# Stick-breaking attention on one NeuronCore: the carries of both heads in the two halves of one tile, and the work of a unit in one row

## The chip, the cores and the metric

The kernel runs on one NeuronCore of a Trainium2 chip. The time is the device time of one execution in microseconds (us); where several executions were timed, their median is given. The profile is of one further execution, and its span runs from that execution's first instruction to its last.

The engines are named as in the profile: PE multiplies matrices (PEld is the loading of its stationary operand), DVE is the vector engine, ACT the scalar engine, POOL the general engine, and SP issues most of the transfers.

## The reference, cut to what matters

The kernel computes one decoder block on 1024 rows of width 1024: a state-space branch and an attention branch, joined by gates, and a feed-forward part. The change lies in the attention of 8 heads with 64 dimensions each, of which this is the core:

```python
z = jnp.einsum('bhqd,bhkd->bhqk', qb, kh) * scale
mask = key_pos < q_pos
log_not = jnp.where(mask, jax.nn.log_sigmoid(-z), 0.0)
suffix = lax.cumsum(log_not, axis=3, reverse=True) - log_not
weights = jnp.where(mask, jnp.exp(jax.nn.log_sigmoid(z) + suffix), 0.0)
return jnp.einsum('bhqk,bhkd->bhqd', weights, vh)
```

So a weight needs the sum of `log_not` over all keys that lie behind it. The kernel goes through the keys from the last to the first and hands the sum so far from one block of 128 keys to the next. That handed-on sum is what the code keeps in the tiles `row0` and `row1`; it is called the carry here.

## The kernel before, in words

Before the attention come the projections and the state-space branch (to about 345 us of the span), after it the output projection of the branch and the gates (`branch_b`, from about 642 us), the output matrix, and the feed-forward part. The program is built by a framework that orders the instructions of DVE, ACT, POOL and SP by its own estimate of times. The matrix products of the attention are kept in the order in which the code writes them: all of them go through `pinned` (line 838), so in the profile the line of every one of them is L838, and they are told apart by the names of their tiles.

The attention goes through four pairs of heads. Of each pair, the 64 dimensions of one head lie in rows 0 to 63 of the operands `q` and `k`, those of the other in rows 64 to 127. Of each pair there are two groups of 512 queries (Q = 0 and 1), and each group goes through its blocks of keys from the last to the first, three units in the first group and seven in the second: 40 units in all. The first unit of a group holds the two last blocks, with 128 and 256 queries behind the mask; the second has 384 queries, all others 512.

A unit passes through three functions, at different times:

- `scores`: products of `k` and `q` into the PSUM tile `z`, one per head (64 rows each). Then a copy on ACT (L920), or on DVE with the mask added (L918) for the three blocks on the diagonal, and on ACT and DVE the steps to `ws`, which DVE splits into a high part `wh` (L925) and a rest `wl` (L926), in fp32r, the rounded float format in which one pass of PE suffices.
- `sums`: for each head two products of `upto`, a triangle of ones, with `wh` and `wl` into the PSUM tile `acc`, and, from a group's second unit on, one product of `ones` with the carry. The carry tile holds 128 rows and both heads beside each other, [128, 2, 512]. Only two of its rows are not zero: row 0 (high part) and row 32 (rest), so that one product with all 128 rows of ones adds both. Then the new carry is taken from row 0 of `acc`: ACT writes its high part for both heads in one instruction (L947), DVE subtracts `acc` from the scores of each head (L949, twice) and writes the rest of the carry for both heads (L951). The tile `acc` is there once, so the next unit's sums wait for L951. ACT then takes the exponential (L952), which gives the weights `wa`.
- `values`: products of the weights and `V` into a PSUM tile named `mm`, one per head, 64 columns of the array each.

PE doesn't run these alone. Between them stand products of other projections (the next heads' `q` and `k`, the gates), called fillers, by counts in `FILL`. In the loop of `attention`, step i writes: the sums of unit i, 8 fillers, the values of unit i-1, the scores of unit i+3, 8 fillers. In the last three steps there are no scores any more, and 8 and 6 fillers. For the fillers, POOL splits weights into high parts and rests (L458, L459).

Of the kernel before, what the change touches and what calls it, by code (L numbers as in the profile page):

```python
# [9 lines left out]
F32 = mybir.dt.float32  # L10
F32R = mybir.dt.float32r
I32 = mybir.dt.int32
AF = mybir.ActivationFunctionType
ALU = mybir.AluOpType
# [350 lines left out]
P = 128  # L365
# [12 lines left out]
LOOK = 3  # L378
FILL = (8, 8, 12, 6)
# [50 lines left out]
class Block:  # L430
# [497 lines left out]
    def sums(self, u, work):  # L928


        nc, g, a, f = self.nc, u.group, u.a, u.f
        kb, fs, c = u.segs[-1]
        past = g.row
        r = self.accp.tile([P, 2, 512], F32, name="acc")
        for x in range(2):
            for n in range(2):
                self.pinned(r[:, x, 0:f], lhsT=self.upto, rhs=u.parts[n][:, x, 0:f], start=n == 0, stop=False)
            if past is None:
                for n in range(2):
                    self.pinned(r[:, x, f - P:f], lhsT=self.ones_r, rhs=u.parts[n][:, x, 0:P], start=False, stop=n == 1)  # L940
        if past is not None:
            old = slice(c.start + P if kb >= 4 * u.Q else 0, 512)
            for x in range(2):
                self.pinned(r[:, x, old.start - c.start:f], lhsT=self.ones_r, rhs=past[:, x, old], start=False, stop=True)
        if kb:
            g.row = self.rows.tile()
            nc.scalar.copy(g.row[0:1, :, c], r[0:1, :, fs])  # L947
        for x in range(2):
            nc.vector.tensor_tensor(a[:, x, 0:f], a[:, x, 0:f], r[:, x, 0:f], ALU.subtract)  # L949
        if kb:  # L950
            nc.vector.tensor_tensor(g.row[32:33, :, c], r[0:1, :, fs], g.row[0:1, :, c].bitcast(F32), ALU.subtract)  # L951
        self.last_exp = nc.scalar.activation(a[:, :, 0:f], a[:, :, 0:f], AF.Exp)  # L952

    def values(self, u, out):
# [9 lines left out]
    def attention(self, qk, qp, kp, vp, op, gp, rowp, part, work, cp):  # L964


        nc = self.nc
        units, ops = [], []
        carries = []
        for n in range(RWB):  # L970
            t = rowp.tile([P, 2, 512], F32R, name=f"row{n}")
            carries.append(t)
        self.rows = Again(carries)
        for hp in range(4):
# [6 lines left out]
        def some(n):  # L981
            for _ in range(n):
                next(fill, None)

        V = None
        for i in range(-LOOK, len(units) + 1):
            if 0 <= i < len(units):
                self.sums(units[i], work)
                some(FILL[0])
            if i > 0:  # L990
                u = units[i - 1]
                if u.group.av is None:
                    if u.Q == 0:
                        V = vp.tile([P, KT, P], F32, name="V")
                        nc.sync.dma_start(out=V, in_=self.vD.rearrange("(t p) d -> p t d", p=P)[:, :, P * u.hp:P * u.hp + P])
                        ops.append(op.tile([P, 1024], F32, name="o"))
                    u.group.V = V
                    u.group.av = self.avp.tile([P, 512], F32, name="mm")
                self.values(u, ops[u.hp])
            if i + LOOK < len(units):  # L1000
                self.scores(units[i + LOOK], qk, part, work)
                if i == -LOOK:
                    for t in carries:
                        self.after(nc.vector.tensor_scalar(t.rearrange("p a (b c) -> p (a b) c", c=P), self.ident.unsqueeze(1).broadcast_to([P, 8, P]), 0.0, None, ALU.mult), self.masked)
                some(FILL[1] if i >= 0 else FILL[2])
            elif i < len(units):
                some(FILL[3])
        some(10000)
        return ops

# [607 lines left out]
```

## Time and profile before

| | |
|---|---|
| median of three runs | 1433.7 us (1431.09 to 1435.74) |
| profiled execution, its own time | 1436.13 us |
| its span | 1434.4 us |
| PE busy | 1408.1 us, 98% of the span |
| DVE busy | 1078.4 us, 75% |
| ACT busy | 639.9 us, 45% |
| POOL busy | 514.5 us, 36% |
| granted clock of PE | 0.996 |

The view of stretches gives the busy time of each engine between two times; the timeline gives instructions in order, those of a kind that follow each other merged with their number (x2); the view of groups gives for each form its count, its busy time and the mean duration of one, and behind the bar the idle time just before them. A product of two f32 operands shows as two instructions, one of two fp32r operands as one. On PE the durations of neighbours overlap, so a product's price is read from one start to the next, not from its duration.

### The profile page before, as it was taken

Reading aid. Unit: us, or ns where it says so; the run is one execution under the profiler, and the core shown is the slowest. Engines: PE = TensorE matmul, PEld = TensorE weight load, DVE = VectorE, ACT = ScalarE, POOL = GpSimd, SP = SyncE. Lnnn points to the kernel's source line nnn. Section 1 sums busy time; section 2 is a strip of 40 time slices with the busy share of each in tenths; the row PEclk is TensorE's granted clock in tenths of the full one; section 3 lists DMA queues with packets and bytes.
Section 4 is the critical chain, followed back from the end, with each engine's and each line's share of the span. In section 5 each row is a group of like instructions: output and inputs, shape, how many; then the busy total and the mean of one; then the engine's idle time right before and its main releaser. Section 6 shows DMA issues by size and latency. Waiting matters only on the chain.

```text
span 1434.4 us, 18472 instructions
## 1 busy us (share of the span) xinstructions
PE 1408.1 (98%) x6821; PEld 1121.3 (78%) x6821; DVE 1078.4 (75%) x1388; ACT 639.9 (45%) x852; POOL 514.5 (36%) x288
## 2 busy tenths in 40 slices
PE   8899999998999999999999999999999999999997
PEld 6689888887666666668888888888888888788886
DVE  5679985656897989877824697877667667799896
ACT  4433324423777776774328442332323233433335
POOL 1020000102101111104400017776767666699394
PEclk9999999999999999999999999999999999999999
DMA  9656667299011112217533234444444359899722
GB/s 338 170 136 178 161 161 213 69 334 310 16 52 52 44 30 81 66 38 240 190 121 118 68 91 152 167 139 162 140 162 138 117 198 386 287 370 364 253 81 117
DMA packets 193274, 233.41 MB, mean 163 GB/s; under 512 B 29468, under 2 KB 128864, under 8 KB 193184
## 3 DMA queue, kind: packets, MB, share of 16 engines
q1 hardware_dynamic: 184048, 224.70, 47.8%
q10 hardware_dynamic: 8912, 7.48, 1.9%
q8 instruction: 54, 0.88, 0.3%
q14 instruction: 36, 0.29, 0.1%
q0 software_dynamic: 224, 0.05, 0.0%
HBM read 162.85 MB, written 68.16 MB: 161 GB/s over the span
## 4 chain that ended last, share of the span: by engine, by line
PE 80%; DVE 9%; DMA 5%; ACT 3%; issue 2%; POOL 1%; SPq 0%; ACTq 0%; POOLq 0%; DVEq 0%
PE tq L1308 12%; PE wo L1308 6%; PE tq L1429 6%; PE mm L1308 6%; PE mx L838 5%; PE mm L838 5%; PE mm L767 4%; PE mm L1429 3%; PE mx L767 3%; PE wo L1429 3%; PE acc L838 2%; PE wo L1145 2%; PE mm L1145 2%; PE mm L664 2%; PE z L838 2%
## 5 line engine op out<-in xcount | busy, mean ns | idle before, releaser
L475 POOL TENSOR_TENSOR ws<-wb 128x1024 f32<-128x1024 f32 x24 | 60.6, 2526 | 171.4 <-DVE wl L478 142.7
L459 POOL TENSOR_TENSOR wl<-ws,wh 128x1024 fp32r<-128x1024 f32 x12 | 31.4, 2616 | 151.4 <-ACT wh L456 150.9
L949 DVE TENSOR_TENSOR wa<-wa,acc 128x512 f32<-128x512 f32 (+1 forms) x80 | 47.0, 628 | 31.0 <-ACT row L947 28.8
L1355 POOL TENSOR_TENSOR pa<-pa 128x512 f32<-128x512 f32 x30 | 63.3, 2136 | 0.3
L1299 POOL TENSOR_TENSOR f<-f,f 128x512 f32<-128x512 f32 x30 | 53.1, 1795 | 26.1 <-DVE f L1293 18.9
L921 ACT ACTIVATE ws<-wa 128x1024 f32<-128x1024 f32 (+1 forms) x40 | 39.0, 976 | 47.6 <-DVE wa L918 47.2
L926 DVE TENSOR_TENSOR wl<-ws,wh 128x1024 fp32r<-128x1024 f32 (+1 forms) x40 | 56.3, 1407 | 1.0
L478 DVE TENSOR_TENSOR wl<-ws,wh 128x1024 fp32r<-128x1024 f32 x23 | 40.8, 1775 | 19.2 <-ACT wh L477 19.1
L1030 DVE SCALAR_TENSOR_TENSOR acc<-aw,cond,acc 128x512 f32<-128x512 f32 x56 | 45.7, 817 | 9.1 <-DMA aw<-in_w_ada_dram 8.4
L1384 POOL TENSOR_TENSOR pa<-pa,row 128x1024 f32<-128x1024 f32 x14 | 43.7, 3135 | 15.5 <-DMA pa<-in_w_ffn_down_dram 15.5
L924 DVE SCALAR_TENSOR_TENSOR ws<-wa,ws 128x1024 f32<-128x1024 f32 (+1 forms) x40 | 45.5, 1137 | 4.3 <-ACT ws L923 3.4
L1292 ACT ACTIVATE f<-f 128x1024 f32<-128x1024 f32 x20 | 21.2, 1061 | 60.6 <-DVE f L1330 31.4
L952 ACT ACTIVATE wa<-wa 128x1024 f32<-128x1024 f32 (+1 forms) x40 | 38.8, 971 | 19.7 <-DVE wa L949 18.7
L838 PE MATMUL z<-q,k 64*128 64x512 f32 (+3 forms) x192 | 41.8, 527 | 4.4 <-DVE na L1095 2.6
L477 ACT CAST wh<-ws 128x1024 fp32r<-128x1024 f32 x23 | 24.2, 1054 | 49.1 <-PE wo L1308 15.5
L456 ACT CAST wh<-ws 128x1024 fp32r<-128x1024 f32 x24 | 25.1, 1048 | 44.2 <-PE wo L1145 21.1
L458 POOL TENSOR_SCALAR wh<-ws 128x1024 fp32r<-128x1024 f32 x6 | 7.2, 1205 | 103.5 <-issue 36.1
L477 ACT CAST wh<-wb 128x1024 fp32r<-128x1024 f32 x25 | 26.2, 1051 | 40.4 <-PE mm L1429 9.7
L475 POOL TENSOR_TENSOR wgs<-wb 128x1024 f32<-128x1024 f32 x12 | 28.9, 2407 | 41.4 <-DVE wl L478 20.3
L1429 PE MATMUL tq<-f,f 128*128 128x512 f32 x136 | 41.7, 389 | 0.0
L838 PE MATMUL mm<-wa,V 128*64 128x512 f32 (+3 forms) x192 | 39.8, 507 | 0.0
L478 DVE TENSOR_TENSOR wl<-wb,wh 128x1024 fp32r<-128x1024 f32 x25 | 38.3, 1536 | 1.9 <-ACT wh L477 1.9
(849 smaller groups left out, 4701.6 us busy)
## 6 DMA issues: line engine op xcount, KB each, us to landing
wb<-hD SPq DMA_DIRECT2D x40, 512.0 KB, 5.6
aw<-in_w_ada_dram SPq DMA_DIRECT2D x64, 256.0 KB, 4.4
hD<-f SPq DMA_DIRECT2D x30, 512.0 KB, 5.1
ws<-in_w_in_dram SPq DMA_DIRECT2D x23, 512.0 KB, 4.6
wb<-in_w_ffn_gate_dram SPq DMA_DIRECT2D x44, 256.0 KB, 4.4
wb<-in_w_ffn_up_dram SPq DMA_DIRECT2D x44, 256.0 KB, 4.8
ws<-hD SPq DMA_DIRECT2D x20, 512.0 KB, 6.0
x<-in_x_dram SPq DMA_DIRECT2D x16, 512.0 KB, 7.4
```

What stands on the lines that cost most here:

```text
L475: (add or nc.gpsimd).tensor_tensor(st, a, b, op)
L477: nc.scalar.copy(h, a)
L478: self.last_lo = (lo or nc.vector).tensor_tensor(l, a, h.bitcast(F32), ALU.subtract)
L767: self.nc.tensor.matmul(ps, lhsT=w[a][:, k], rhs=act[h][k][:, b], start=(j == 0), stop=(j == n - 1))
L838: return self.tc.keep_in_program_order(self.nc.tensor.matmul(*args, **kw))
L926: nc.vector.tensor_tensor(lt, st, ht.bitcast(F32), ALU.subtract)
L949: nc.vector.tensor_tensor(a[:, x, 0:f], a[:, x, 0:f], r[:, x, 0:f], ALU.subtract)
L1145: self.nc.tensor.matmul(ps, lhsT=mg[t // 4][k][:, a, P * (t % 4):P * (t % 4) + P], rhs=ws[k // 2][b][:, k % 2], start=k + j == 0, stop=k + ...
L1299: self.last_sum = nc.gpsimd.tensor_tensor(o, a, b, op)
L1308: self.nc.tensor.matmul(ps, lhsT=w[x][:, q, k], rhs=self.B[i](y, k), start=(j == 0), stop=(j == 11))
L1355: self.after(nc.gpsimd.tensor_tensor(t[:, n], part(a), part(b), SIGN_B[i]), first)
L1429: nc.tensor.matmul(ps, lhsT=o[x][:, P * t:P * t + P], rhs=o[y][:, R], start=(j == 0), stop=(j == 3 * np_ - 1))
```

## The change

The carry tile becomes [128, 512]. Head 0 has its carry in rows 0 (high part) and 32 (rest), head 1 in rows 64 and 96. The product of a head's carry takes only that half of the rows of the carry and of `ones`, so it has 64 rows instead of 128, the form that the scores have. ACT's copy and DVE's rest are written per head, two instructions where there was one. In the loop, the scores of unit i+3 follow directly on the sums of unit i, then the values of unit i-1, then all 16 fillers (14 in the last three steps).

```diff
         if past is not None:
             old = slice(c.start + P if kb >= 4 * u.Q else 0, 512)
             for x in range(2):
-                self.pinned(r[:, x, old.start - c.start:f], lhsT=self.ones_r, rhs=past[:, x, old], start=False, stop=True)
+                h = slice(64 * x, 64 * x + 64)
+                self.pinned(r[:, x, old.start - c.start:f], lhsT=self.ones_r[h], rhs=past[h, old], start=False, stop=True)
         if kb:
             g.row = self.rows.tile()
-            nc.scalar.copy(g.row[0:1, :, c], r[0:1, :, fs])
+            for x in range(2):
+                nc.scalar.copy(g.row[64 * x:64 * x + 1, c], r[0:1, x, fs])
         for x in range(2):
             nc.vector.tensor_tensor(a[:, x, 0:f], a[:, x, 0:f], r[:, x, 0:f], ALU.subtract)
-        if kb:
-            nc.vector.tensor_tensor(g.row[32:33, :, c], r[0:1, :, fs], g.row[0:1, :, c].bitcast(F32), ALU.subtract)
+            if kb:
+                q = 64 * x
+                nc.vector.tensor_tensor(g.row[q + 32:q + 33, c], r[0:1, x, fs], g.row[q:q + 1, c].bitcast(F32), ALU.subtract)
...
-            t = rowp.tile([P, 2, 512], F32R, name=f"row{n}")
+            t = rowp.tile([P, 512], F32R, name=f"row{n}")
...
             if 0 <= i < len(units):
                 self.sums(units[i], work)
-                some(FILL[0])
+            if i + LOOK < len(units):
+                self.scores(units[i + LOOK], qk, part, work)
...
                 self.values(u, ops[u.hp])
             if i + LOOK < len(units):
-                self.scores(units[i + LOOK], qk, part, work)
...
-                some(FILL[1] if i >= 0 else FILL[2])
+                some(FILL[0] + FILL[1] if i >= 0 else FILL[2])
             elif i < len(units):
-                some(FILL[3])
+                some(FILL[0] + FILL[3])
```

Three lines are added, so the names move: L947, L949, L951 and L952 of before are L949, L951, L954 and L955 after the change.

On PE, in the middle of the attention (a unit with 512 queries), the order changes as follows. `mx` and `mm` with `wgh`, `wgl` are fillers, `mm` with `wa` and `V` are values:

```order
 L838 MATMUL acc<-wl,upto 128x512
 L838 MATMUL acc<-row_3618,ones 128x512 x2
+L838 MATMUL z<-q,k 128x512 x2
+L838 MATMUL mm<-wa,V 64x512 x2
 L838 MATMUL mx<-pb,wgh 128x512 x2
 L838 MATMUL mx<-pb,wgl 128x512
@@ -1212,6 +1212,4 @@
 L838 MATMUL mx<-pb,wgl 128x512
 L838 MATMUL mx<-pb,wgh 128x512 x2
-L838 MATMUL mm<-wa,V 64x512 x2
-L838 MATMUL z<-q,k 128x512 x2
 L838 MATMUL mx<-pb,wgl 128x512
 L838 MATMUL mx<-pb,wgh 128x512 x2
```

The scores, which came last between the fillers, now stand right behind the carry, and the values behind the scores.

On PE at the end of the attention, in the last unit, there are no scores left to follow the carry. After the change it reads:

```order
L838 MATMUL acc<-wl,upto 128x512
L838 MATMUL acc<-row_3617,ones 128x512 x2
L838 MATMUL mm<-wa,V 64x512 x2
L838 MATMUL mx<-pa,wl 128x512
L838 MATMUL mx<-pa,wh 128x512 x2
```

Here the carry, with 64 rows, stands between products of 128 rows and values of 64 columns; before, it stood between two kinds of products of the full array.

On DVE, near the end of a group, before the change (L949 the subtraction, L951 the carry's rest, L918 the mask for the next group):

```order
L949 TENSOR_TENSOR wa<-wa,acc 128x512 x2
L951 TENSOR_TENSOR row_3618<-acc,row_3618 1x1024
L924 SCALAR_TENSOR_TENSOR ws<-wa,ws 128x1024
L918 TENSOR_TENSOR wa<-z,mask 128x2x384
L925 TENSOR_SCALAR wh<-ws 128x1024
```

and a unit later in the changed kernel (there L951 is the subtraction and L954 the carry's rest):

```order
L924 SCALAR_TENSOR_TENSOR ws<-wa,ws 128x2x384
L918 TENSOR_TENSOR wa<-z,mask 128x2x384
L951 TENSOR_TENSOR wa<-wa,acc 128x512
L954 TENSOR_TENSOR row_3617<-acc,row_3617 1x512
L925 TENSOR_SCALAR wh<-ws 128x2x384
L951 TENSOR_TENSOR wa<-wa,acc 128x512
L954 TENSOR_TENSOR row_3617<-acc,row_3617 1x512
```

The subtractions and the rests now alternate by head, and the splitting L925 has come between them here. Before the attention the order of the program is the same on every engine, and after it only a few products, copies and transfers of `branch_b` have changed places.

More of the change, by code (lines that the diff above doesn't have):

```diff
@@ L988, in attention @@
                 self.sums(units[i], work)
-                some(FILL[0])
+            if i + LOOK < len(units):
+                self.scores(units[i + LOOK], qk, part, work)
+                if i == -LOOK:
+                    for t in carries:
+                        self.after(nc.vector.tensor_scalar(t.rearrange("p (b c) -> p b c", c=P), self.ident.unsqueeze(1).broadcast_to([P, 4, P]), 0.0, None, ALU.mult), self.masked)
             if i > 0:
@@ L1000, in attention @@
             if i + LOOK < len(units):
-                self.scores(units[i + LOOK], qk, part, work)
-                if i == -LOOK:
-                    for t in carries:
-                        self.after(nc.vector.tensor_scalar(t.rearrange("p a (b c) -> p (a b) c", c=P), self.ident.unsqueeze(1).broadcast_to([P, 8, P]), 0.0, None, ALU.mult), self.masked)
-                some(FILL[1] if i >= 0 else FILL[2])
+                some(FILL[0] + FILL[1] if i >= 0 else FILL[2])
             elif i < len(units):
-                some(FILL[3])
+                some(FILL[0] + FILL[3])
         some(10000)
```

## The prediction

> **What bounds the kernel now.** I read the page first, its busy times and its chain of waits, then the stretches around the attention.
>
> ```profile
> PE 1408.1 (98%) x6821; PEld 1121.3 (78%) x6821; DVE 1078.4 (75%) x1388; ACT 639.9 (45%) x852; POOL 514.5 (36%) x288
> PE 80%; DVE 9%; DMA 5%; ACT 3%; issue 2%; POOL 1%; SPq 0%; ACTq 0%; POOLq 0%; DVEq 0%
> ```
>
> ```profile
> core 0: us, PE busy (x) PEld busy (x) DVE busy (x) ACT busy (x) POOL busy (x), PEclk, DMA share, GB/s
> 380.00:640.00 260.00, 258.29 (x1181) 169.84 (x1180) 221.04 (x252) 192.24 (x218) 33.74 (x16) 1.00 0.16 50
> 640.00:662.00 22.00, 22.00 (x100) 17.38 (x100) 9.73 (x15) 9.42 (x15) 1.71 (x2) 1.00 0.62 205
> 662.00:702.00 40.00, 39.42 (x174) 32.30 (x172) 38.93 (x37) 18.65 (x28) 23.74 (x12) 1.00 0.47 157
> ```
>
> PE carries the end, and in the stretch that the change touches it is idle for 1.7 of 260 us. So what PE is spared there shortens the kernel, as long as nobody else becomes the last. The nearest is DVE with 221 of 260 us (85%), then ACT with 74%.
>
> The timeline of PE over one unit of 512 queries shows what a unit costs:
>
> ```profile
> 474.42 0.62 PE L838 MATMUL acc<-row,ones 128*128 128x512 f32 x2
> 474.88 0.40 PE L838 MATMUL mm<-pa,wh 128*128 128x512 f32 x1
> ...
> 476.49 0.39 PE L838 MATMUL mm<-pa,wl 128*128 128x512 f32 x1
> 476.81 1.08 PE L838 MATMUL mm<-wa,V 128*64 128x512 f32 x4
> 477.81 1.13 PE L838 MATMUL z<-q,k 64*128 64x512 f32 x4
> 478.87 0.73 PE L838 MATMUL mm<-pa,wh 128*128 128x512 f32 x2
> 479.44 0.40 PE L838 MATMUL mm<-pa,wl 128*128 128x512 f32 x1
> 479.68 0.62 PE L838 MATMUL mm<-pa,wh 128*128 128x512 f32 x2
> ...
> 480.82 0.39 PE L838 MATMUL acc<-wh,upto 128*128 128x512 f32 x1
> ...
> 481.73 0.62 PE L838 MATMUL acc<-row,ones 128*128 128x512 f32 x2
> 482.19 0.40 PE L838 MATMUL mm<-pa,wl 128*128 128x512 f32 x1
> ```
>
> From start to start the unit takes 481.73 - 474.42 = 7.31 us. The two carries take 0.46, 0.23 each. Where the form of the array's use changes (128*128, 128*64, 64*128), it costs something: the last filler before the values takes 0.32 instead of 0.23, and the first two after the scores 0.57 instead of 0.46, that is 0.09 and 0.11.
>
> **The carries side by side.** How many there are and how wide:
>
> ```profile
> L838 PE MATMUL acc<-row,ones 128*128 128x512 f32 x32 | 10.0, 393 | 0.0
> L838 PE MATMUL acc<-row,ones 128*128 128x384 f32 x16 | 4.1, 338 | 0.0
> L838 PE MATMUL acc<-row,ones 128*128 128x256 f32 x16 | 3.2, 279 | 0.0
> ```
>
> ```profile
> 509.90 0.40 PE L838 MATMUL acc<-row,ones 128*128 128x256 f32 x2
> 510.13 0.63 PE L838 MATMUL mm<-pb,wh 128*128 128x512 f32 x2
> ...
> 516.59 0.51 PE L838 MATMUL acc<-row,ones 128*128 128x384 f32 x2
> 516.94 0.40 PE L838 MATMUL mx<-pa,wgh 128*128 128x512 f32 x1
> ```
>
> So one carry costs 0.23, 0.175 and 0.115 us, and there are 16, 8 and 8 pairs. If the two of a pair run at the same time, each pair costs one of them: 16 x 0.23 + 8 x 0.175 + 8 x 0.115 = 3.68 + 1.40 + 0.92 = 6.0 us gone. Do they? The scores have the form that the carries get, 64 rows per head and a PSUM tile in two parts. Their four instructions of 512 columns take 1.06 us. What four would take one after the other is bounded by passes of the same format on the full array:
>
> ```profile
> L1194 PE MATMUL tq<-ident,row x16: 272/273/273, 766.8 to 801.9; 128*128 128x128 f32 x16
> 755.24 0.44 PE tq L1194 x4
> ```
>
> 128 columns take 0.11 us, 512 so 0.44, and four of them 1.76. The scores need 1.06, so they do run in pairs. The carries are in fp32r, where the trace has 0.115 us for 256 columns, twice the speed of these f32 passes. That two halves of the array also overlap at this speed no row shows: both ends are open, a gain of 6.0 and a gain of 0. I take 6.0, since the scores' pairs are the nearest row, and keep 0 for the range.
>
> The Trainium skill bears on how complete the overlap is. Its page "TensorE: Matmul & The Clock Gate", Part 3, measures four row tiles of 32 rows with 512 columns at 3.07 times one, not 4. By that share, as an estimate from the page, two tiles would gain 1.54 times, a pair of 512 would cost 0.30 instead of 0.23 us, and the sum of the pairs would be 4.2 instead of 6.0 us. The scores' rows can't tell this from the cost of changing the form.
>
> **The order on PE.** Before, a unit changes the form three times: fillers to values, values to scores, scores to fillers. After, it changes it three times as well: sums to carry, scores to values, values to fillers, since carry and scores have the same form. I take nothing for that. Were each pair of carries to pay a change of its own, it would be 32 x (0.09 + 0.11) = 6.4 us, which is why carry and scores stand together. This cover is missing in the last three units, which have no scores: there the carry stands alone, at 3 x 0.20 = 0.6 us lost.
>
> **Copies and rests per head.** The rows of the old and the new shapes:
>
> ```profile
> L947 ACT CAST row<-acc 1x1024 fp32r<-1x1024 f32 x16 | 15.9, 991 | 2.4 <-PE acc L838 2.3
> L947 ACT CAST row<-acc 1x512 fp32r<-1x512 f32 x7 | 3.9, 558 | 0.0
> L951 DVE TENSOR_TENSOR row<-acc,row 1x1024 fp32r<-1x1024 f32 x16 | 19.4, 1215 | 0.5
> L951 DVE TENSOR_TENSOR row<-acc,row 1x512 fp32r<-1x512 f32 x7 | 4.8, 680 | 0.2
> L949 DVE TENSOR_TENSOR wa<-wa,acc 128x512 f32<-128x512 f32 x46 | 29.4, 681 | 10.4 <-ACT row L947 8.2 <-PE acc L838 2.2
> ```
>
> ACT needs 2 x 0.56 = 1.12 instead of 0.99 us, DVE 2 x 0.68 = 1.36 instead of 1.215. Over 32 units that is at most 4.2 us on ACT and 4.6 on DVE, in 260 us in which DVE rests for 39. It lies beside PE and I take nothing; without that cover it would be the 4.6. What is behind it matters more: the sums of the next unit need `acc` free, so they wait for the last rest. A tight case is this unit, in which a DVE split takes 3.20 us while POOL works:
>
> ```profile
> 473.75 2.41 POOL L459 TENSOR_TENSOR wgl<-wgs,wgh 128x1024 fp32r<-128x1024 f32 x1 [18.37 <-ACT wgh L456]
> 474.04 3.20 DVE L926 TENSOR_TENSOR wl<-ws,wh 128x1024 fp32r<-128x1024 f32 x1
> 475.63 0.99 ACT L947 CAST row<-acc 1x1024 fp32r<-1x1024 f32 x1
> 477.16 1.27 DVE L949 TENSOR_TENSOR wa<-wa,acc 128x512 f32<-128x512 f32 x2
> 478.46 1.21 DVE L951 TENSOR_TENSOR row<-acc,row 1x1024 fp32r<-1x1024 f32 x1
> ```
>
> The rest ends at 479.67, the next sums start at 480.82: 1.15 us to spare. After the change the copies take 0.13 and the four DVE pieces (4 x 0.68 = 2.72 against 2.48) 0.24 more, and the stretch from carry to next sums holds the same fillers, values and scores: about 0.8 us to spare. Twice before, it did not suffice:
>
> ```profile
> 536.70 3.25 POOL L459 TENSOR_TENSOR wgl<-wgs,wgh 128x1024 fp32r<-128x1024 f32 x1
> 537.72 2.78 DVE L925 TENSOR_SCALAR wh<-ws 128x1024 fp32r<-128x1024 f32 x1
> 544.82 0.47 PE L838 MATMUL acc<-wh,upto 128*128 128x512 f32 x1 [1.21 <-DVE row L951]
> L838 PE MATMUL acc<-wl,upto 128*128 128x512 f32 x48 | 18.8, 392 | 0.5 <-DVE wl L926 0.5
> ```
>
> These 1.7 us of waiting may go (the changed order puts the splits L925 and L926 behind the subtractions in more units) or come again elsewhere (near a group's end the mask L918 stands ahead of the subtraction, and waits there for scores that PE now makes sooner). Bounds: 1.7 gained, 4.6 lost, the whole new DVE work. I take 0.4 lost, near the gain because the spare time of an ordinary unit covers the longer chain.
>
> **The sum.** 6.0 - 0.6 - 0.4 = 5.0 us less on PE. It passes through to the end: after the attention DVE has 12 of 22 us idle until 662, then is full until 702 (38.9 of 40), but its work there starts from PE's products, so both move ahead together. The profiled execution took 1436.13 us with a span of 1434.4; that becomes 1431.1 and 1429.4. The median of the runs lies 2.4 us below the profiled execution, so the forecast is 1433.7 - 5.0 = 1428.7 us.
>
> **The rivals.**
>
> 1. The pairs overlap only in part, because half arrays at fp32r speed share something that the slower scores don't. For it: no row shows the case. Against it: nothing in the rows either. With half of the 6.0 left the gain is 3.0 - 1.0 = 2.0, so 1431.7. By the Trainium skill's share above (same page and Part) it would be 4.2 - 1.0 = 3.2, so 1430.5, an estimate.
> 2. They don't overlap at all: 0 - 1.0, so 1434.7. The scores' rows speak against it.
> 3. The release of `acc` decides: four alternating DVE pieces, with the mask ahead of them in places, end later than the next sums want `acc`, and PE waits. It decides once more than 5.0 us of such waits are added. In the stretch from 380 to 640 POOL has 16 instructions; two waits of PE stand in it now, 0.85 us on average. If a dozen more of the meetings cost that, it is 10.2 us: 1433.7 - 5.4 + 10.2 = 1438.5, slower than before. The spare 0.8 us speaks against it.
> 4. The gain is taken back after the attention, because a transfer or DVE's full stretch to 702 doesn't move with PE: 1433.5. Against it: DVE and ACT are under half busy from 640 to 662.
>
> **How the numbers follow.** Less than 0.3% (4.3 us) can't be told from no change in a measurement of this kernel. Chances: forecast 0.58, rival 1 0.15, rival 2 0.09, rival 3 0.12, rival 4 0.06. The forecast's own spread is about 2 us (the waits of -1.7 to +2, and the scatter of runs), 1426 to 1431, so 0.7 of it is faster than 1429.4: 0.41. A fifth of rival 1 adds 0.03, and a gain above 6.0, by waits that go, is in it: 0.45. Slower needs over 1438.0: over half of rival 3 and some of rival 2, 0.10. Same is the rest, 0.45. The range is 1425.5 to 1436: it leaves out the long waits of rival 3 and little else.
>
> **What would show it.** In the timeline after: the two carries of a pair start within 0.02 us of each other, and the scores follow 0.23 us later; a unit of 512 queries takes 7.08 instead of 7.31 us; the last three units have carries alone, with the added 0.2. Wrong: carries 0.2 us apart (rival 2), scores over 0.3 us after them (rival 1), PE idle before `acc<-wh,upto` released by DVE L954 in more than five units (rival 3), a wait after 662 that was not there (rival 4).

## The result and the profile after

| | before | after |
|---|---|---|
| median of four runs each | 1432.39 us | 1444.58 us (1443.2 to 1444.96) |
| ratio | | 1.0081, 95% interval 1.0068 to 1.0094 |
| profiled execution, its own time | 1436.13 us | 1444.48 us |
| its span | 1434.4 us | 1442.8 us |

The change makes the kernel 12 us slower; 5 us faster was forecast, and the range ended at 1436. The page of the changed kernel, its busy times and its chain of waits:

```profile
PE 1407.2 (98%) x6821; PEld 1115.1 (77%) x6821; DVE 1079.3 (75%) x1420; ACT 646.3 (45%) x884; POOL 511.5 (35%) x288
PE 67%; DVE 13%; ACT 7%; issue 6%; DMA 4%; POOL 3%; SPq 1%; DVEq 0%; POOLq 0%; ACTq 0%
```

PE is busy for 1 us less than before, and its share of the chain falls from 80% to 67%; the shares of DVE (9% to 13%), ACT (3% to 7%), POOL (1% to 3%) and of "issue", time in which the engine of the chain waited for nothing that the profile shows (2% to 6%), grow. The view of stretches says where:

```profile
380.00:640.00 260.00, 248.31 (x1142) 158.71 (x1140) 215.37 (x270) 193.14 (x241) 32.64 (x16) 0.99 0.15 46
```

In the attention PE is idle for 11.7 of 260 us, where it was 1.7. The timeline of PE over a unit:

```profile
475.66 0.47 PE L838 MATMUL acc<-wh,upto 128*128 128x512 f32 x1 [0.54 <-DVE row L954]
...
476.42 0.39 PE L838 MATMUL acc<-wl,upto 128*128 128x512 f32 x1
476.74 0.50 PE L838 MATMUL acc<-row,ones 64*128 64x512 f32 x2
477.08 1.02 PE L838 MATMUL z<-q,k 64*128 64x512 f32 x4
478.03 1.08 PE L838 MATMUL mm<-wa,V 128*64 128x512 f32 x4
...
484.08 0.50 PE L838 MATMUL acc<-wh,upto 128*128 128x512 f32 x1 [1.09 <-DVE row L954]
484.42 0.40 PE L838 MATMUL acc<-wl,upto 128*128 128x512 f32 x1
```

The pair of carries does run side by side: both have ended 0.50 us after the first began, and the scores start 0.34 us behind the first carry, where before the change the next product started 0.46 us behind it. But the sums of this unit waited 0.54 us, and those of the next wait 1.09 us, for DVE's rest of the carry, L954. After a wait the products also come slower for a moment: 0.34 instead of 0.23 us from the first to the second. The view of waits from 360 to 645 us, of the changed kernel:

```profile
ACT wa L955 <- DVE wa L951: 47.5, 27, 4.1
DVE ws L924 <- ACT ws L923: 38.8, 29, 3.1
PE acc L838 <- DVE row L954: 13.1, 13, 2.2
```

and of the kernel before (us in total, number, longest):

```profile
ACT wa L952 <- DVE wa L949: 18.7, 19, 3.0
DVE ws L924 <- ACT ws L923: 1.9, 4, 0.6
PE acc L838 <- DVE row L951: 1.2, 1, 1.2
```

The second line of each is the one to look at. Before, L924 hardly waited for the logarithm L923. Now it waits 29 times, 38.8 us, and what stands behind L924 on DVE starts only after it. What stands there is seen in the timeline of DVE, ACT and POOL, put together here:

```profile
472.72 0.68 DVE L951 TENSOR_TENSOR wa<-wa,acc 128x512 f32<-128x512 f32 x1
...
474.11 0.69 DVE L951 TENSOR_TENSOR wa<-wa,acc 128x512 f32<-128x512 f32 x1
...
474.83 1.06 ACT L955 ACTIVATE wa<-wa 128x1024 f32<-128x1024 f32 x1 [0.89 <-DVE wa L951]
...
475.80 1.04 ACT L922 ACTIVATE ws<-ws 128x1024 f32<-128x1024 f32 x1
...
476.74 1.04 ACT L456 CAST wgh<-wgs 128x1024 fp32r<-128x1024 f32 x1
477.68 1.05 ACT L923 ACTIVATE ws<-ws 128x1024 f32<-128x1024 f32 x1
477.86 2.39 POOL L459 TENSOR_TENSOR wgl<-wgs,wgh 128x1024 fp32r<-128x1024 f32 x1 [19.43 <-ACT wgh L456]
...
478.77 2.56 DVE L924 SCALAR_TENSOR_TENSOR ws<-wa,ws 128x1024 f32<-128x1024 f32 x1 [1.40 <-ACT ws L923]
...
481.25 0.67 DVE L951 TENSOR_TENSOR wa<-wa,acc 128x512 f32<-128x512 f32 x1
481.94 0.68 DVE L954 TENSOR_TENSOR row<-acc,row 1x512 fp32r<-1x512 f32 x1
482.63 0.69 DVE L951 TENSOR_TENSOR wa<-wa,acc 128x512 f32<-128x512 f32 x1
...
488.42 0.68 DVE L951 TENSOR_TENSOR wa<-wa,acc 128x512 f32<-128x512 f32 x1
```

Read it as a ring. The second subtraction L951 (474.11) lets the exponential L955 go; behind the exponential on ACT stand L922 and L923 of a unit three later; L923 lets L924 go; behind L924 on DVE stand the next unit's subtractions and rests. From the first subtraction of one unit to that of the next it takes 481.25 - 472.72 = 8.53 us here, with a filler's cast (L456) in the ring and an L924 of 2.56 us, and 488.42 - 481.25 = 7.17 us the next time, without these two but with the split L925 (487.81 to 488.42) between L924 and the subtraction. Without L925 it would be 6.56 us. PE's unit, where nothing waits, is 7.09 us. So the bare ring is shorter than a unit, and what falls into it makes it longer. In the kernel before this ring isn't closed: there the exponential stood behind L923, and L924 behind the rest. Another one is seen in its timeline, over the exponential, L920, L921, L922 and the carry's copy L947 on ACT to the next subtraction: 483.54 - 477.16 = 6.38 us, against a unit of 7.31.

To see what the waits cost, I took the starts of all instructions of PE from the first sums to the last values. What lies from one start to the next is counted as idle time (the earlier instruction had ended), as restart (what the step into a wait and the two steps behind it take over the median step of their kind), as the step from one carry of a pair to the other, or as the rest.

| us | stretch | waits (number) | restarts | second carries | rest |
|---|---|---|---|---|---|
| before | 278.0 | 1.7 (2) | 0.5 | 6.0 | 269.8 |
| after | 289.7 | 13.5 (17) | 4.6 | 0.1 | 271.5 |

The carries give 5.9 us. The waits with their restarts take 15.9 more than before. The rest is 1.8 longer. Over half of that, 1.1, is PE's clock, which fell to half behind the longest wait. Here are the view of stretches (the column behind POOL's is the granted clock), and the timeline, where steps of 0.23 us take 0.43:

```profile
551.00:554.00 3.00, 3.00 (x8) 1.63 (x9) 1.81 (x2) 2.40 (x3) 0.00 (x0) 0.50 0.00 0
554.00:556.00 2.00, 2.00 (x10) 0.58 (x7) 1.88 (x4) 1.92 (x4) 0.00 (x0) 1.00 0.11 31
```

```profile
550.65 0.77 PE L838 MATMUL acc<-wh,upto 128*128 128x512 f32 x1 [2.24 <-DVE row L954]
551.21 0.63 PE L838 MATMUL acc<-wl,upto 128*128 128x512 f32 x1
551.64 0.63 PE L838 MATMUL acc<-wh,upto 128*128 128x512 f32 x1
```

The stretch is 11.7 us longer, near the 12.2 of the medians; the two spans differ by 8.4, since the kernel before entered the attention 3 us later in its profile.

### The profile page after: what moved, and what is told of

Read it like the earlier page. It is cut to its first block, busy times and chain, and to the rows that moved or that the text cites. A ratio compares the mean times of both kernels' runs of the same rounds, so it can differ in the third digit from the quotient of the medians.

```text
span 1442.8 us, 18586 instructions
## 1 busy us (share of the span) xinstructions
PE 1407.2 (98%) x6821; PEld 1115.1 (77%) x6821; DVE 1079.3 (75%) x1420; ACT 646.3 (45%) x884; POOL 511.5 (35%) x288
## 4 chain that ended last, share of the span: by engine, by line
PE 67%; DVE 13%; ACT 7%; issue 6%; DMA 4%; POOL 3%; SPq 1%; DVEq 0%; POOLq 0%; ACTq 0%
PE tq L1311 11%; PE wo L1311 6%; PE tq L1432 6%; PE mm L1311 5%; PE ga L767 5%; PE mm L767 4%; PE mx L767 3%; PE mm L1432 3%; PE wo L1432 3%; DVE wa L951 3%; PE wo L1148 2%; PE mm L1148 2%; PE mm L664 2%; DVE row L954 2%; ACT ws L923 2%
## 5 line engine op out<-in xcount | busy, mean ns | idle before, releaser
L924 DVE SCALAR_TENSOR_TENSOR ws<-wa,ws 128x1024 f32<-128x1024 f32 (+1 forms) x40 | 52.7, 1318 | 40.8 <-ACT ws L923 40.8
L955 ACT ACTIVATE wa<-wa 128x1024 f32<-128x1024 f32 (+1 forms) x40 | 38.9, 973 | 50.5 <-DVE wa L951 50.2
L951 DVE TENSOR_TENSOR wa<-wa,acc 128x512 f32<-128x512 f32 (+1 forms) x80 | 49.6, 628 | 2.6 <-PE acc L838 1.8
L926 DVE TENSOR_TENSOR wl<-ws,wh 128x1024 fp32r<-128x1024 f32 (+1 forms) x40 | 49.2, 1229 | 0.9
L921 ACT ACTIVATE ws<-wa 128x1024 f32<-128x1024 f32 (+1 forms) x40 | 39.0, 974 | 24.2 <-DVE wa L918 23.8
L838 PE MATMUL acc<-wh,upto 128*128 128x512 f32 (+1 forms) x80 | 32.6, 407 | 13.5 <-DVE row L954 13.1
L456 ACT CAST wh<-ws 128x1024 fp32r<-128x1024 f32 x24 | 25.1, 1047 | 42.6 <-PE wo L1148 21.1
L1130 POOL TENSOR_TENSOR gb<-gb,ma 128x512 f32<-128x512 f32 x7 | 11.8, 1681 | 84.7 <-DMA ma<-nD 73.9
```

Of the source, the lines that this page charges most:

```text
L838: return self.tc.keep_in_program_order(self.nc.tensor.matmul(*args, **kw))
L924: nc.vector.scalar_tensor_tensor(st, a, 0.0, st, ALU.max, ALU.add)
L926: nc.vector.tensor_tensor(lt, st, ht.bitcast(F32), ALU.subtract)
```

## The experiments

Times are medians; each ratio is to the kernel before, run beside it on the same chip. That kernel took 1431.8 to 1433.0 us in these rounds, so times of different rounds are compared as they are.

### One part of the change alone

The half-row carries, in the loop's old order:

```diff
-                self.pinned(..., lhsT=self.ones_r, rhs=past[:, x, old], ...)
+                self.pinned(..., lhsT=self.ones_r[h], rhs=past[h, old], ...)
...
             (copies and rests per head, as in the change; the loop of before)
```

> The first part of the change alone: the carries of the two heads in two halves of one tile, with copies and rests per head, while the loop keeps its order of before (sums, 8 fillers, values of the last unit, scores, 8 fillers). Theory (the order of the work on DVE and ACT, which the moved scores turned round, makes PE wait for acc; the half-row carries are sound): on DVE and ACT the order is that of before, so PE waits for acc for about 2 us as before, not 15. The pairs save 6.0 us; each of 32 pairs now pays a change of form on both sides of its own, 0.2 to 0.4 us, 6 to 12 us in all. So 1433 to 1440 us, with PE idle before acc<-wh,upto in at most five units. Rival (the split copies and rests, four alternating pieces on DVE, are what holds acc): PE waits for acc for 10 us or more here too, and the time is 1443 to 1450 us.

Measured: 1441.56 us, ratio 1.006 (1.0043 to 1.0077). The theory's waits are right: PE waits four times, 3.3 us. The waits of this kernel:

```profile
ACT wa L955 <- DVE wa L951: 29.1, 25, 2.8
PE acc L838 <- DVE row L954: 2.7, 3, 1.2
DVE ws L924 <- ACT ws L923: 1.0, 2, 0.8
```

So split copies and rests in the old order hardly make PE wait (a unit is also 0.15 us longer here than before, 7.45 us, which gives them more cover). Of the 9 us, 7 come from changes of form: the second carries take 0.1 instead of 6.0 us, and the rest of the stretch 282.7 instead of 269.8, 12.9 more for 32 pairs, 0.40 each. The other 2 are waits with restarts, 4.4 us against 2.2. Its timeline shows the three places (0.32, 0.43 and 0.34 from start to start, against 0.23):

```profile
479.84 0.39 PE L838 MATMUL acc<-wl,upto 128*128 128x512 f32 x1
480.16 0.50 PE L838 MATMUL acc<-row,ones 64*128 64x512 f32 x2
480.59 0.50 PE L838 MATMUL mm<-pa,wl 128*128 128x512 f32 x1
480.93 0.63 PE L838 MATMUL mm<-pa,wh 128*128 128x512 f32 x2
```

For these changes 6 to 12 us were expected; it is a little over the upper end, and so is the time, by 1.6 us.

The row order alone, with the full-row carries of before:

```diff
                 self.sums(units[i], work)
-                some(FILL[0])
+            if i + LOOK < len(units):
+                self.scores(units[i + LOOK], qk, part, work)
...
-                some(FILL[1] if i >= 0 else FILL[2])
+                some(FILL[0] + FILL[1] if i >= 0 else FILL[2])
```

> The second part alone: sums, scores and values of a unit in a row, then all fillers; the carries stay in full rows as before, with one copy and one rest for both heads. Theory (the moved scores turn the order on DVE and ACT round): DVE has L924 of a unit two ahead before the subtractions, as in the changed kernel, PE waits for acc by 10 us or more, nothing is saved on the pairs: 1443 to 1450 us. Rival (the split copies and rests are what holds acc): waits as before, about 2 us, and a time of 1431 to 1436 us.

Measured: 1435.73 us, ratio 1.0019 (1.0009 to 1.003). The time lies at the upper end of the rival's range, and my theory's is missed by 7 us; but the waits are not those of before. L924 does wait for L923 as in the changed kernel,

```profile
DVE ws L924 <- ACT ws L923: 35.6, 27, 3.7
PE acc L838 <- DVE row L951: 4.6, 5, 1.1
```

but PE loses only 7.1 us in waits and restarts (5.1 and 2.0). So the turned order is a cause, and it isn't the whole: the two parts together lose 18.1, the row order alone 7.1, the half rows alone 4.4, and the kernel before 2.2. Each part alone adds 2 to 5 us, both together 15.9: the split copies and rests, which cost little in the old order, cost most in the row.

### Orders forced on DVE and ACT

L924 and the splits of unit i+2 behind the last rest of unit i:

```diff
-        nc.vector.scalar_tensor_tensor(st, a, 0.0, st, ALU.max, ALU.add)
+        ins = nc.vector.scalar_tensor_tensor(st, a, 0.0, st, ALU.max, ALU.add)
+        if first is not None:
+            self.after(ins, first)
...
+                if i + 2 < len(units):
+                    self.split_parts(units[i + 2], self.last_sub)
```

> The changed kernel with one order more: on DVE, L924 of unit i+2 has to stand behind the last rest of the carry of unit i, where it stood before the change. The work is the same. Theory that L924 ahead of the subtractions is what makes them late: PE's waits for acc fall from 13 to under 4 us and the time to 1428 to 1434 us. Rival (the loop is held on ACT, where the exponential now comes ahead of the scores' steps, or by DVE's work as a whole): waits of 8 us or more stay and the time is 1438 us or more.

Measured: 1440.45 us, ratio 1.0051 (1.0036 to 1.0066): 4 us of the 12 back. The theory's time is missed by 6 us and more; the rival's figures, 1438 us or more and waits of 8 or more, came (10.1 us in all). The waits for `acc` fall to 6.0 us, but PE now waits elsewhere, for the scores' tile, which DVE's mask frees late:

```profile
PE acc L838 <- DVE row L961: 5.2, 7, 1.6
PE z L838 <- DVE wa L918: 4.4, 6, 2.4
...
PE acc L838 <- DVE wl L933: 0.8, 1, 0.8
```

The exponential behind L923 of unit i+3 on ACT:

```diff
-        self.last_exp = nc.scalar.activation(a[:, :, 0:f], a[:, :, 0:f], AF.Exp)
+    def weights(self, u):
+        self.last_exp = self.nc.scalar.activation(u.a[:, :, 0:u.f], u.a[:, :, 0:u.f], AF.Exp)
+        self.after(self.last_exp, self.last_ln)
```

> The changed kernel with another order more: on ACT the exponential of unit i has to stand behind L923, the logarithm of unit i+3, so the scores' steps no longer wait on ACT behind an exponential that itself waits for the subtractions on DVE. The work is the same. Theory that the waits come from a loop over both engines (subtraction on DVE, exponential, L922 and L923 on ACT, L924 on DVE, next subtraction) of nearly a unit's length: with the exponential out of it the loop is over 2 us shorter, PE's waits for acc fall under 4 us, and the time is 1427 to 1432 us. Rival (DVE's own work, four pieces per unit, is what is late): waits of 8 us or more stay, and the time is 1438 us or more.

Measured: 1459.79 us, ratio 1.0181 (1.0166 to 1.0196). The ring is cut and the kernel is 15 us slower still; the theory's time is missed by 28 us, and the waits for `acc` stay over the rival's 8 us. Most of the waiting is new: the weights now come too late for the values, which the row order wants right behind the next sums:

```profile
PE mm L838 <- ACT wa L958: 15.9, 11, 3.1
PE acc L838 <- DVE row L954: 8.9, 9, 2.3
```

So I gave the weights a unit more, with the scores two units ahead instead of three and the exponential still held behind the logarithm, without and with the subtractions ahead of the rests:

```diff
-LOOK = 3
+LOOK = 2
...
-                u = units[i - 1]
+                u = units[i - 2]
```

> The changed kernel, but the values come two units behind the sums instead of one, the scores two units ahead instead of three (so as many weights are kept), and on ACT the exponential of unit i has to stand behind the logarithm of unit i+2. Nothing on ACT waits for the subtractions any more ahead of the scores' steps, and the weights have a unit more before PE wants them. Theory (the loop from subtraction over exponential, logarithm and L924 to the next subtraction makes PE wait): waits for acc fall under 5 us with their restarts, no new waits for the weights, 1428 to 1433 us. Rival (DVE and ACT are too full in this stretch for a unit of 7.08 us, in whatever order): waits of 10 us or more, 1438 us or more.

> As the kernel before it (values two units behind, scores two ahead, the exponential behind the next logarithm), and the two subtractions ahead of the two rests. Theory: the loop is cut already, so the turns no longer count: within 2 us of the kernel before it, 1428 to 1433 us. Rival (the turns count by themselves, whatever the loop): 3 us or more faster than it.

Measured: 1460.55 us (ratio 1.0162 to 1.0202) and 1458.46 us (1.0141 to 1.0191). Both miss the theory's 1428 to 1433 by 25 us and more, and the difference of 2.1 us lies between the two expectations of the second. The waits for weights are gone, but the splits are late instead (the first of the two kernels):

```profile
PE acc L838 <- DVE wl L926: 7.8, 10, 1.7
PE acc L838 <- DVE row L954: 6.3, 5, 2.8
PE acc L838 <- DVE wh L925: 4.4, 2, 3.5
```

These forced orders each move a wait, and none shows by itself what the ring costs; taken alone they speak for the rival, that DVE and ACT are too full for a unit of 7.08 us in any order. The last kernels below, which hold such a unit nearly without waits, speak against it. What the forced orders do show is that the row order leaves little room on either side.

### The length of the ring

The two subtractions ahead of the two rests, which lets the exponential go 0.68 us sooner; the work is the same, and the last rest stays the last:

```diff
         for x in range(2):
             nc.vector.tensor_tensor(a[:, x, 0:f], a[:, x, 0:f], r[:, x, 0:f], ALU.subtract)
-            if kb:
+        if kb:
+            for x in range(2):
                 q = 64 * x
```

> The changed kernel with the two subtractions ahead of the two rests, instead of in turns, so that the exponential, which needs both subtractions, no longer waits for head 0's rest (0.68 us) and through it for ACT's copy. The work is the same, and the last rest ends no sooner. Theory (the turns make the difference between the changed kernel, with 18 us of waits, and the row order alone, with 7, because they sit in the loop from subtraction to exponential to the next unit's scores to L924 to the next subtraction): waits fall to 7 to 9 us and the time to 1432 to 1436 us. Rival (what counts is when the last rest ends, and that PE's unit has become 0.23 us shorter): PE waits for 15 us or more with their restarts, 1441 us or more.

Measured: 1438.65 us, ratio 1.0043 (1.003 to 1.0055), between the two: 5.9 us less than the changed kernel. Waits and restarts are 14.1 instead of 18.1 us, nearer the rival's 15 than the theory's 7 to 9. The longest wait is 1.4 us, and the clock keeps 1.00 in this stretch: the rest of the stretch is 269.6, as before the change.

One tile of `acc` per head instead, so that head 0's sums needn't wait for head 1's rest:

```diff
-        r = self.accp.tile([P, 2, 512], F32, name="acc")
+        r = [self.accp.tile([P, 512], F32, name=f"acc{x}") for x in range(2)]
```

> The changed kernel with the tile acc cut into one tile per head, of the same size together, so that the sums of head 0 wait only for the rest of head 0. The work is the same. Theory (what PE waits for is the last rest in acc): only the two products of head 0, 0.46 us, can be done before head 1's rest is needed, so each of the 13 waits for acc shrinks by up to 0.46 us and some vanish: 5 to 8 us of idle time less, 1436 to 1440 us. Rival (the engines behind PE set the pace as a closed loop, and a release that comes sooner for one head gives nothing, because the subtractions themselves are late): 1443 us or more.

Measured: 1443.0 us, ratio 1.0072 (1.0045 to 1.0098), with 16.3 us of waits and restarts, as the rival had it. A sooner release of half of `acc` gives nothing clear of the scatter; a sooner exponential gives 6 us. That speaks for the ring against the tile.

The rests left out altogether, so that the carry is handed on with its rounded high part alone:

```diff
-                nc.vector.tensor_tensor(g.row[q + 32:q + 33, c], r[0:1, x, fs], g.row[q:q + 1, c].bitcast(F32), ALU.subtract)
```

> The changed kernel without L954: the rest of the carry is left out, so the carry is handed on with its rounded high part alone, and the two subtractions follow each other. Of the loop this takes 0.68 us between the subtractions, and of DVE 1.36 us per unit. Theory (loop and DVE's work make PE wait): PE's waits for acc fall to 2 to 5 us with their restarts, 1427 to 1432 us. Rival (ACT's chain of exponential, L922, L923 ahead of the next L924 sets the pace alone): waits of 8 us or more, 1435 us or more.

Measured: 1426.62 us, ratio 0.9958 (0.9942 to 0.9973). Waits and restarts fall to 2.8 us, the rest is 269.3: with 1.36 us less work on DVE per unit, and 0.68 less in the ring, the forecast's gain is there. This kernel leaves out part of the sum, so it shows a cause and is no remedy.

### A shorter unit on PE

One filler less per unit, in the kernel before and in the changed one (the fillers left over come behind the attention):

```diff
-FILL = (8, 8, 12, 6)
+FILL = (8, 7, 12, 6)
```

> The kernel before with 15 instead of 16 fillers between a unit and the next, that is 0.23 us less of PE's work per unit, some 8.5 us over 37 units; the fillers left over come behind the attention, so the work is the same. This asks what a shorter unit on PE is worth in the order of before. From the first sums to the last values it was 278.0 us. If DVE and ACT have room (PE was idle for 1.7 us only): the stretch shrinks by 7 to 9 us, to 269 to 271, and the time stays within 3 us of 1432.5. If they are at their limit in this order too: the stretch stays at 275 us or more and the time grows by 5 us or more, to 1437 or above.

> The changed kernel with 15 instead of 16 fillers per unit, as in the run before it. From the first sums to the last values it took 289.7 us, of which PE waited 18 with the restarts. Theory (in the row order a loop over DVE and ACT sets the pace, not PE): the stretch stays within 3 us of 289.7, all that PE saves becomes waiting, and the fillers left over lengthen the time by 6 to 10 us, to 1450 to 1455. Rival (PE sets the pace, and the waits are meetings by chance): the stretch shrinks by 6 us or more, and the time stays at 1442 to 1447 us.

Measured: the kernel before 1430.18 us, ratio 0.998 (0.9966 to 0.9993), its stretch 267.6 with no wait at all. So the order of before has room for a shorter unit. The changed kernel: 1445.81 us, ratio 1.0091 (1.0062 to 1.0121), in the rival's range. In the profiled execution, which took 1440.70 us and so 5.1 less than the median, the stretch shrank by 10.0 to 279.7, with 16.5 us of waits and restarts as against 18.1. Both contradict my theory: a ring that set the pace of every unit would have kept the stretch. The waits are single meetings in some units. The bare ring of 6.56 us above fits this, for it is shorter than this unit too (7.09 less one filler's 0.23, so 6.86); how long the ring is in each unit I didn't measure.

### What makes the ring late

In the timeline above, L924 took 2.56 us beside an instruction of POOL, twice its usual time. So I looked at all instructions of DVE from 360 to 640 us that took over 0.3 us more than the shortest of their form: 11 before, 12 after, and each of them overlaps one of POOL's. The sum of what they lose is the same, 16.1 and 15.2 us. But before, they are L925 (3), L926 (7) and L924 (1); after, L924 (7), L925 (2) and L926 (3). The row order alone has 13, nine of them L924, and they lose 17.5 us; yet that kernel loses 7.1 us only to waits and restarts. So a slowed L924 ahead of the subtractions is not enough by itself. The groups of these lines, before:

```profile
L926 DVE TENSOR_TENSOR wl<-ws,wh 128x1024 fp32r<-128x1024 f32 x24 | 38.0, 1584 | 0.6
L924 DVE SCALAR_TENSOR_TENSOR ws<-wa,ws 128x1024 f32<-128x1024 f32 x24 | 30.2, 1257 | 1.6 <-ACT ws L923 0.9
```

and after:

```profile
L924 DVE SCALAR_TENSOR_TENSOR ws<-wa,ws 128x1024 f32<-128x1024 f32 x24 | 35.2, 1467 | 31.2 <-ACT ws L923 31.2
L926 DVE TENSOR_TENSOR wl<-ws,wh 128x1024 fp32r<-128x1024 f32 x24 | 31.4, 1308 | 0.6
```

Nor is it L924 alone. Before the longest wait, 2.24 us at 550.65, the slowed instruction is an L926 behind the subtractions of the unit before, the place that the prediction called a tight case. From there DVE works without a break through L890, L924, L925 and the four pieces to the last rest:

```profile
541.99 3.28 DVE L926 TENSOR_TENSOR wl<-ws,wh 128x1024 fp32r<-128x1024 f32 x1
...
549.82 0.68 DVE L954 TENSOR_TENSOR row<-acc,row 1x512 fp32r<-1x512 f32 x1
```

The Trainium skill, "SBUF — State Buffer", "SBUF: two separate sides", says that a port pair which DVE and the GpSimd engine (POOL) share is an exclusive lock, held for a whole instruction, and that the other engine blocks; DVE needs it for an operation with two inputs in SBUF, as L924 and L926 have, or in certain fast modes. The trace agrees: POOL's instruction ended at 477.86 + 2.39 = 480.25, L924 at 481.33, 1.08 us later, which is near L924's whole time alone (1.22).

To take it away, the fillers' weights are split on ACT and DVE instead of POOL:

```diff
-            loaded.append(self.w3(self.weight(..., lo_eng=nc.gpsimd, hi_eng=nc.gpsimd if n == "g" else None, ring=rings[turn % 3])))
+            loaded.append(self.w3(self.weight(..., lo_eng=nc.vector, hi_eng=None, ring=rings[turn % 3])))
```

> The changed kernel with the fillers' weights split on ACT and DVE instead of POOL (their high part on ACT, their rest on DVE), so that no instruction of POOL runs beside DVE's in the attention. DVE gets some 14 instructions of 1.2 us more, ACT 7 of 1.05. Theory (the longest waits stand where POOL's split makes one of DVE's instructions in the loop take 2.4 to 3.2 us instead of 1.2): waits of over 1.5 us go, the waits fall by 4 to 8 us, and the time to 1436 to 1441 us. Rival (DVE and ACT are full as it is, and the work moved to them costs what the slowing cost): within 3 us of 1444.6, or above.

Measured: 1432.78 us, ratio 0.9999 (0.9988 to 1.0011). This takes 11.8 us off the changed kernel, more than expected, although DVE and ACT got more work. No instruction of DVE is slowed by over 0.3 us any more, and waits and restarts fall to 7.4 us:

```profile
L924 DVE SCALAR_TENSOR_TENSOR ws<-wa,ws 128x1024 f32<-128x1024 f32 x24 | 29.4, 1223 | 20.7 <-ACT ws L923 20.7
```

The control, the same edit in the kernel before:

> The kernel before with the fillers' weights split on ACT and DVE instead of POOL, the same edit that took 11.8 us from the changed kernel. Theory (in the order of before, POOL's slowing falls on L925 and L926, behind the subtractions, where it has room; only the row order puts L924 with its slowing ahead of them): within 3 us of 1432.5, 1430 to 1434. Rival (POOL's slowing costs both kernels the same, and has nothing to do with the change): faster by 6 us or more, 1426 or below.

Measured: 1431.21 us, ratio 0.999 (0.9975 to 1.0005), as the theory had it. The same slowing cost the kernel before 0.6 us by the medians, and at most 3.6 by the interval, as against 11.8 in the changed one. What it costs depends on where it falls.

Both edits that helped, and then with 15 fillers as well:

> The changed kernel with both edits that helped: the fillers' weights split on ACT and DVE (1432.8 us alone), and the two subtractions ahead of the two rests (1438.7 alone, against 1444.6). If both shorten the same loop, what is left of the waits (7.4 us with restarts) falls to 2 to 5 us: 1427 to 1431 us, under both kernels. If the waits that are left are of another kind: 1432 us or more.

> The kernel before this one with 15 instead of 16 fillers per unit. In the order of before this took 2.3 us off, in the changed kernel it added 1.2 us. If the loop has room again: within 2 us of the run before it, or up to 3 us less. If it is at its limit, waits return: 3 us or more above it.

Measured: the first 1426.77 us, ratio 0.9959 (0.9945 to 0.9973), 5.0 us under the 1431.8 of the kernel before beside it. This version lies under both kernels, 4.4 us under the kernel before with the same splits, and computes the whole. PE's waits in it, and a unit of 512 queries in its timeline, 7.09 us from carry to carry:

```profile
PE acc L838 <- DVE row L955: 1.6, 4, 0.8
```

```profile
469.41 0.50 PE L838 MATMUL acc<-row,ones 64*128 64x512 f32 x2
...
476.50 0.50 PE L838 MATMUL acc<-row,ones 64*128 64x512 f32 x2
```

The second: 1431.0 us, ratio 0.9988 (0.9977 to 1.0). There the shorter unit does bring waits back, 6.3 us with restarts instead of 3.1, so DVE and ACT are near their limit again.

The runs side by side, in us (the kernels with forced orders on ACT are left out). The times are medians, all other columns are of the profiled execution; it lies within 2.2 us of the median, but 5.1 below it for "after, 15 fillers":

| | time | stretch | waits (number) | restarts | second carries | rest |
|---|---|---|---|---|---|---|
| half rows alone | 1441.6 | 287.2 | 3.3 (4) | 1.1 | 0.1 | 282.7 |
| row order alone | 1435.7 | 281.8 | 5.1 (7) | 2.0 | 6.0 | 268.7 |
| L924 behind the rests | 1440.5 | 286.4 | 10.1 (13) | 5.8 | 0.1 | 270.5 |
| one `acc` per head | 1443.0 | 288.4 | 11.0 (16) | 5.2 | 0.1 | 272.0 |
| rests last | 1438.7 | 283.9 | 10.7 (12) | 3.4 | 0.1 | 269.6 |
| no rests | 1426.6 | 272.3 | 1.6 (5) | 1.2 | 0.1 | 269.3 |
| before, 15 fillers | 1430.2 | 267.6 | 0.0 (0) | 0.0 | 6.0 | 261.6 |
| after, 15 fillers | 1445.8 | 279.7 | 12.3 (16) | 4.2 | 0.1 | 263.1 |
| splits on DVE | 1432.8 | 277.9 | 5.3 (8) | 2.1 | 0.1 | 270.5 |
| before, splits on DVE | 1431.2 | 276.5 | 0.5 (1) | 0.3 | 6.0 | 269.8 |
| splits on DVE, rests last | 1426.8 | 272.7 | 1.8 (5) | 1.3 | 0.1 | 269.5 |
| the same, 15 fillers | 1431.0 | 267.8 | 4.7 (6) | 1.6 | 0.1 | 261.4 |

## Why the prediction was wrong, step by step

**The pairs, 6.0 us: right.** The second carries fell from 6.0 to 0.1 us, and a unit of 512 queries without a wait takes 7.09 us, where 7.08 was forecast. Rival 2 is out. The sign given for rival 1, scores over 0.3 us behind the carries, did come: 0.33 us. But it doesn't mean a partial overlap here. The scores start 0.33, 0.28 and 0.22 us behind carries of 512, 384 and 256 columns, each time 0.10 more than one carry alone, and an overlap in part would cost the wide pairs more than the narrow ones. It is a step between two forms, counted next, and rival 1 is out too.

**The changes of form, nothing (0.6 in the last units): right as a sum, by parts that cancel.** Not three steps cost, but four: the carry starts 0.32 us behind the sums instead of 0.23, and the scores 0.33 behind the carry, though both use 64 rows, so "carry and scores have the same form" doesn't make that step free. In return the scores take 0.95 instead of 1.06 us, and the 0.09 from fillers to values is gone. Where the row order had few or short waits, the rest of the stretch is 269.3 to 269.6 us, as against 269.8 before.

**Copies and rests, nothing by themselves: right in the old order alone.** There they come with 4.4 us of waits and restarts instead of 2.2 (first experiment). In the row they don't lie beside PE any more: 18.1 us with them, 7.1 without. The unit is also 0.2 us shorter with them, but a further 0.23 less, with 15 fillers, added no waits (16.5 us).

**The waits for `acc`, 0.4 us lost: this step failed.** With the restarts it was 15.9 us, and 1.1 of halved clock on top. The failing sentence is that an ordinary unit has "about 0.8 us to spare". It took DVE's order from the kernel before, with two corrections in length, 0.13 and 0.24 us. But the moved scores turn that order round: L924 of a unit two later, fed by ACT behind the exponential, now stands ahead of the subtractions. The listing of DVE's order ahead of the prediction has it, L924 and L918 above L951; I read from it that L925 had gone behind the subtraction, and not that a wait for ACT had come ahead of it. I also used the 3.20 us beside POOL as the tight case for an L926 behind the subtractions, and didn't ask what happens when the slowed one stands directly ahead of them, nor what DVE then still has to do: behind the L926 of 3.28 us at 541.99 it was L890, L924, L925 and four pieces.

**Rival 3 came, for 0.12.** Its name was right, PE waits for the last rest; its price of 10.2 us was too low, since 15 waits came on top of the two instead of a dozen, and each costs its restart too, 0.27 us on average (4.6 over 17). Its mechanism, four alternating pieces with the mask ahead, was part of it: setting the rests last gave 5.9 us back. The larger part, 11.8 us, needs POOL's slowing of instructions on DVE; the rival counted meetings with POOL, but not where they fall. Which of the slowed instructions cost how much, the runs don't part: seven were L924, and the longest wait stands behind an L926. The two edits together give 17.8 us, and with them the change is worth the 5.0 us that were forecast, 4.4 of them against the kernel before with the same splits. That the forecast's number comes out then is in part luck: in the stretch the pairs give 5.9 us, waits and restarts take 0.9 more, and the steps between forms, with four instead of three, happen to cancel.

**It passes to the end: right.** PE's wait at 702.09 us before the change stands at 710.43 after it, 8.3 later, as the span is 8.4 longer. Rival 4 is out.

What stays open: how much of the waiting goes through the ring and how much through DVE's work as a whole, for the ring was read from timelines and the edits that helped shorten both. Of the 5.3 us of waits that are left with the splits on DVE, 2.6 stand at two group ends (at 421.99 and 492.45 us), where the mask L918 comes ahead of the subtractions and L925 between them, and 1.1 behind a filler's split that now lies on DVE, ahead of L924. Whether a row order with the scores or weights further apart and more room for their tiles would do as well is open too; I didn't try more room.

## What to carry to other kernels

When products move on an engine whose order is written in the code, look at the engines whose order is not: list what now stands ahead of each instruction that frees a tile, and follow each such row to what it waits for, until you come back to the start. If that way round is nearly as long as a unit, whatever falls into it can become a wait; here the same slowing cost 0.6 us in one order and 11.8 in the other. A change that shortens the unit of the bounding engine also shortens the cover of everything that hid beside it, so price the cover anew in the changed order, not in the old one.

## What the runs showed of the hardware that I had not expected

- Two products on the two halves of the rows overlap wholly in fp32r: 3 ns from start to start, and the pair costs the time of one, 0.23 us at 512 columns, plus what the changes of form cost: 0.40 us around a pair that stands alone between full products.
- The step from the fp32r carries to the f32 scores, 64 rows each, costs 0.10 us as well. Whether the number format or something else makes it, no run shows.
- Behind some waits PE's granted clock is 0.50 for a while: 3 us behind one of 2.24 us in the changed kernel. With 15 fillers it fell behind one of 1.60 us (0.50 from 374.6 to 378.0). The kernel before had a wait of 2.59 us at 350 us and kept 1.00. The Trainium skill, "TensorE: Matmul & The Clock Gate", Part 1, gives an idle window of about 3.4 us that runs freely; that waits of such length sometimes fall into it and sometimes not would agree with a free window, but the clock fell here after idle times shorter than that.
